# Decoder block on one core: pair operands summed by accumulating transfers, two branch units interleaved, operand work spread over six plain feed-forward pairs

## The chip, the cores and the metric

The kernel runs on one core of a Trainium2 chip. The metric is the device time of one execution in microseconds; before the change it is 979.95 us, the median of 3 runs (978.97 to 980.76). TensorE is called PE here, its weight loads PEld, VectorE DVE, ScalarE ACT, GpSimd POOL, and SP is SyncE, which only issues transfers.

## What is computed

One hybrid decoder block for 512 tokens of width 1024, with 16 learned meta tokens in front (528 columns in all):

```python
xn   = rmsnorm(h, norm1_g)
proj = xn @ w_in            # mq mk mv mi mf mo | gq gk gv ga gr | gate_m gate_g
mqk  = silu(causal_depthwise_conv(concat(mq, mk)))
y_m  = head_rmsnorm(mlstm_chunkwise(mq, mk, mv, logi, logf)) * sigmoid(mo)
y_g  = head_rmsnorm(gla_chunked(gq, gk, gv, loga)) * silu(gr)
merged = sigmoid(gate_m) * (y_m @ w_branch_m) + sigmoid(gate_g) * (y_g @ w_branch_g)
h  = h + merged @ w_out
hn = rmsnorm(h, norm2_g)
h  = h + (silu(hn @ w_ff_gate) * (hn @ w_ff_up)) @ w_ff_down
out = rmsnorm(h, final_g)
```

## The kernel before

**Layout and precision.** Features lie on the 128 partitions and tokens along the free dimension. The big products are made in float32r, as three passes: each operand is split into a high part (a cast on ACT) and a low part (operand minus high part, a subtraction on DVE), and `mm3` (lines 298 to 303) issues high x high, high x low and low x high. The low part of a weight tile is made in `wlo` (L192), the high part in `whi` (L187).

**Units and pairs.** A unit is one weight tile of 1024 x 128, so 8 steps k of `mm3`. `job_list` (L52) writes out the order of all units by hand: gates; four heads of mq, mk, mv, mv, mo, mo; then gm, the GLA projections gq, gk, gv, gr, the branches bm and bg, gg, out, the feed-forward units fg and fu, and down. Some jobs are pairs (`pair`, L350): two weight tiles at once by a scheme of seven half-size products in place of eight, named q1, q5, q6, p2, p3, p4, p7 (`seven`, L339). A pair is 84 matmuls of 256 columns (272 with the meta tokens), where two plain units have 48 of 512. The product p3 of a pair is left pending and issued inside the next job (`left`, `PENDING`, L305). In the feed-forward stage the first NSTD = 5 pairs of fg and fu are plain units, the other 17 are pairs.

**Who sets the order.** The program is unrolled, and each engine works through its own instructions in the order in which they were written. Side work is held in Python generators (`side`, and `mixers` of which only the first runs). After each k of a unit, and after every second k of a pair's product, `tick` (L152) lets every generator go one step; `yield n` means that the generator goes on n ticks later. So a generator's yields decide where among the matmuls its ACT, DVE and DMA instructions stand. `begin` (L270) issues the raw weight load of the fifth unit ahead on SP and places the splits of coming weights at fixed k of the present unit. There are four raw buffers, so a load waits until the low part of an earlier tile is made.

**Operands of the pairs.** A pair needs sums and differences of blocks of the activations, split in two parts. For the mixer's pairs, `normed_x` (L504) makes the normed x from mv 1 on, k by k; `mixed_x` (L520), started at mv 4, adds high and low parts back (L538, L540), forms the sums (L542, L543, L548, L551) and splits them in 272-column halves (`two`, L569: ACT L577, DVE L578 and L575). For the feed-forward pairs, `operands` (L1268) runs from the second unit on: it makes the normed rows `hx` (L1292) and the sums and splits (`two`, L1275), one tick between most steps; the loop at L1345 ticks on until all are there. Weights need such sums as well: accumulating transfers on POOL (L182, L211) make some of them.

**Branches.** `branch_unit` (L1121) runs one unit of bm or bg. Its `need` splits the operand for k and k + 1 just before use (`joined`, `parts`, L838 on ACT and L839 on DVE). Two operands of bg are split earlier, during the last gg pair (`all_parts`, L842). `head_out` (L782) makes these operands per head; its last step is L827.

**Small work on POOL.** `conv` clears three columns there (L704), `mlstm` copies a selector (L862), and `swiglu` (L1251) multiplies there in the plain feed-forward pairs (L1260).

Of the kernel before, what the change touches and what calls it, by code (L numbers as in the profile page):

```python
# [15 lines left out]
P = 128  # L16
D = 1024
KT = 8
# [4 lines left out]
H = 4  # L23
# [22 lines left out]
NSTD = 5  # L46
# [54 lines left out]
def hybrid_block(ctx: ExitStack, tc: tile.TileContext, xT, wst, par, con, out):  # L101
# [35 lines left out]
    X = Box()  # L137

# [131 lines left out]
    def begin(*names):  # L270
# [10 lines left out]
        if all(i[0] == "s" for i in ITEMS[n - 2:n + 1]) and len(names) == 1:  # L281
            n += 1
# [24 lines left out]
    def unit(name, outs, ah, al, need=None):  # L307
# [3 lines left out]
        for k in range(KT):  # L311
            if need is not None:
                need(k)
# [13 lines left out]
    def unit_real(name, ah=None, al=None, need=None):  # L327
# [5 lines left out]
        unit(name, [(o, 0, NS)], ah, al, need)  # L333
# [170 lines left out]
    def normed_x():  # L504

        nh, nl = [], []
        for k in range(KT):
# [4 lines left out]
            S.copy(hi, t)  # L512
            yield 3
# [6 lines left out]
    def mixed_x():  # L520
# [5 lines left out]
        X.w = {n: ([], []) for n in SEVEN}  # L526
        for k in range(4):
            for j in range(2):
                p = (h, l)[j]
                X.w["p2"][j].append(p[k + 4][:, c1])  # L530
                X.w["p3"][j].append(p[k + 4][:, c2])
        three = lambda a: a.rearrange("p (j n) -> p j n", j=2)
        for k in (0, 2):
            t1, t3 = tt(n=2 * HA), tt(n=2 * HA)
            for j in range(2):
                b1, b2 = tt(), tt()
                u1, u3 = three(t1)[:, j], three(t3)[:, j]
                V.tensor_tensor(b1, h[k + j].bitcast(F32), l[k + j].bitcast(F32), ALU.add)  # L538
                yield 1
                V.tensor_tensor(b2, h[k + 4 + j].bitcast(F32), l[k + 4 + j].bitcast(F32), ALU.add)  # L540
                yield 1
                V.tensor_tensor(u1, b1[:, c1], b1[:, c2], ALU.subtract)  # L542
                V.tensor_tensor(u3, b2[:, c2], b1[:, c2], ALU.subtract)  # L543
                yield 1
                two("q5", u1, j)
                yield 1
                two("p7", u3, j)
                V.tensor_tensor(u1, u1, b2[:, c2], ALU.add)  # L548
                yield 1
                two("q6", u1, j, True)  # L550
                V.tensor_tensor(u3, u1, b2[:, c1], ALU.subtract)  # L551
                yield 1
                two("p4", u3, j)
                yield 1
        while unit_ix[0] < UNITS.index(("mo", 7)):
            yield 1
        for k in (0, 2):
            for j in range(2):
                t = tt(F32R, 2 * HA)
                for i in range(2):  # L560
                    c = slice(i * HA, (i + 1) * HA)
                    S.copy(t[:, c], (h, l)[j][k + i][:, c1])
                    X.w["q1"][j].append(t[:, c])
                yield 1
        X.ready = True

    mixed = {}

    def two(n, src, j, neg=False):  # L569
        if j == 0:  # L570
            mixed[n] = tt(F32R, 2 * HA), tt(F32R, 2 * HA)
        hi, lo = (a[:, j * HA:(j + 1) * HA] for a in mixed[n])
        if neg:
            act(hi, src, AF.Copy, scale=-1.0)
            V.scalar_tensor_tensor(lo, src, -1.0, hi.bitcast(F32), ALU.mult, ALU.subtract)  # L575
        else:
            S.copy(hi, src)  # L577
            V.tensor_tensor(lo, src, hi.bitcast(F32), ALU.subtract)  # L578
        X.w[n][0].append(hi)
        X.w[n][1].append(lo)  # L580
# [121 lines left out]
    def conv(box, ps, m, isk):  # L702
        raw = tt(n=TW)
        G.memset(raw[:, 0:3], 0.0)  # L704
# [854 lines left out]
```

## Time and profile before

| | before |
|---|---|
| median of 3 runs | 979.95 us |
| the profiled execution, its own time | 979.11 us |
| its span, first to last instruction | 977.3 us |
| mean granted PE clock | 0.983 |
| DMA, share of 16 engines by queue | hardware 32.5%, software (POOL) 12.7% |

Start of some stages in the profiled execution, in us from the span's start: mv 5 123.0, mo 5 135.6, mo 6 183.3, first gm pair 207, bm 0 299.7, bg 0 511.7, out 0 564, fg 0 608.6, first feed-forward pair 672.9, down 841.6.

The profile's rows name the line of the kernel that issued an instruction, its engine, and its output and inputs by the program's names, so `b<-t,whi` is a matmul into a bank from an activation tile and a weight's high part. "A <- B" in the list of waits says that A stood idle until B was done.

### The profile page before, as it was taken

Reading aid. Unit: us, or ns where it says so; the run is one execution under the profiler, and the core shown is the slowest. Engines: PE = TensorE matmul, PEld = TensorE weight load, DVE = VectorE, ACT = ScalarE, POOL = GpSimd, SP = SyncE. Lnnn points to the kernel's source line nnn. Section 1 sums busy time; section 2 is a strip of 40 time slices with the busy share of each in tenths; the row PEclk is TensorE's granted clock in tenths of the full one; section 3 lists DMA queues with packets and bytes.
Section 4 is the critical chain, followed back from the end, with each engine's and each line's share of the span. In section 5 each row is a group of like instructions: output and inputs, shape, how many; then the busy total and the mean of one; then the engine's idle time right before and its main releaser. Section 6 shows DMA issues by size and latency. Waiting matters only on the chain.

```text
span 977.3 us, 15554 instructions
## 1 busy us (share of the span) xinstructions
PE 926.2 (95%) x6119; PEld 847.9 (87%) x6119; DVE 649.5 (66%) x970; ACT 547.5 (56%) x957; POOL 78.2 (8%) x107
## 2 busy tenths in 40 slices
PE   6999989789999999999998999979999999999995
PEld 6989978778998889999996888858999999988885
DVE  6897787657865567776876555775777777852423
ACT  7557776768865346766873334534555555731321
POOL 0010000001110001101100000012211111000000
PEclk9999998989999999999999999989999999999998
DMA  7342211244563356656642334235777877323302
GB/s 260 102 113 73 87 55 54 65 109 111 139 153 95 97 129 163 158 135 141 140 130 78 105 129 141 65 109 121 193 182 186 187 187 164 109 87 107 107 2 87
DMA packets 43578, 118.64 MB, mean 121 GB/s; under 512 B 4976, under 2 KB 7024, under 8 KB 43504
## 3 DMA queue, kind: packets, MB, share of 16 engines
q1 hardware_dynamic: 31760, 97.19, 32.5%
q0 software_dynamic: 10656, 19.40, 12.7%
q8 instruction: 48, 0.79, 0.3%
q10 hardware_dynamic: 1088, 1.05, 0.3%
q14 instruction: 26, 0.21, 0.1%
HBM read 115.52 MB, written 2.10 MB: 120 GB/s over the span
## 4 chain that ended last, share of the span: by engine, by line
PE 71%; DVE 13%; ACT 12%; issue 2%; DMA 1%; SPq 0%; DVEq 0%; ACTq 0%
PE b L345 11%; PE b L302 11%; PE b L303 11%; PE b L347 11%; PE b L346 11%; PE b L301 11%; ACT t L132 5%; DVE wlo L192 2%; ACT whi L187 2%; ACT L132 1%; DVE t L713 1%; ACT L130 1%; PE b L1046 1%; PE b L1048 1%; DMA t<-xT 1%
## 5 line engine op out<-in xcount | busy, mean ns | idle before, releaser
L302 PE MATMUL b<-t,whi 128*128 128x512 f32 (+2 forms) x806 | 285.3, 354 | 6.3 <-DVE t L839 5.3
L301 PE MATMUL b<-t,whi 128*128 128x512 f32 (+2 forms) x758 | 269.1, 355 | 8.0 <-ACT t L132 6.7
L303 PE MATMUL b<-t,wlo 128*128 128x512 f32 (+2 forms) x758 | 265.8, 351 | 5.2 <-DVE wlo L192 5.2
L345 PE MATMUL b<-t,whi 128*128 128x256 f32 (+1 forms) x888 | 257.0, 289 | 6.7 <-ACT t L405 5.1
L347 PE MATMUL b<-t,wlo 128*128 128x256 f32 (+1 forms) x888 | 252.0, 284 | 0.0
L346 PE MATMUL b<-t,whi 128*128 128x256 f32 (+1 forms) x888 | 251.7, 283 | 0.0
L192 DVE TENSOR_TENSOR wlo<-raw,whi 128x1024 fp32r<-128x1024 f32 x155 | 188.9, 1222 | 52.6 <-ACT whi L187 52.5
L187 ACT CAST whi<-raw 128x1024 fp32r<-128x1024 f32 x155 | 161.6, 1046 | 70.7 <-PE b L346 28.8
L302 PEld LDWEIGHTS b<-t,whi 128*128 128x128 f32 x806 | 153.3, 190 | 29.5 <-DVE t L839 7.5
L345 PEld LDWEIGHTS b<-t,whi 128*128 128x128 f32 x888 | 168.7, 190 | 8.8 <-ACT t L405 6.2
L301 PEld LDWEIGHTS b<-t,whi 128*128 128x128 f32 x758 | 144.9, 191 | 28.1 <-ACT t L132 6.7
L346 PEld LDWEIGHTS b<-t,whi 128*128 128x128 f32 x888 | 168.8, 190 | 0.4
L347 PEld LDWEIGHTS b<-t,wlo 128*128 128x128 f32 x888 | 168.4, 190 | 0.0
L303 PEld LDWEIGHTS b<-t,wlo 128*128 128x128 f32 x758 | 144.4, 191 | 25.2 <-DVE wlo L192 6.1
L132 ACT ACTIVATE t<-t 128x512 f32<-128x512 f32 (+4 forms) x118 | 67.2, 590 | 26.9 <-DVE t L655 6.8
L182 POOL DMA_DIRECT2D raw<-wst x37 | 32.1, 867 | 372.8 <-DMA wf<-wst 107.2
L187 ACT CAST whi<-wf 128x1024 fp32r<-128x1024 f32 x37 | 38.9, 1051 | 21.4 <-PE b L346 14.0
L132 ACT ACTIVATE t<-f 128x256 f32<-128x256 f32 (+1 forms) x24 | 11.6, 481 | 61.7 <-DVE f L1406 61.7
L192 DVE TENSOR_TENSOR wlo<-wf,whi 128x1024 fp32r<-128x1024 f32 x37 | 45.1, 1218 | 0.0
L345 PE MATMUL b<-t,wgh 128*128 128x256 f32 (+1 forms) x148 | 42.5, 287 | 0.0
L347 PE MATMUL b<-t,wgl 128*128 128x256 f32 (+1 forms) x148 | 42.4, 286 | 0.0
L346 PE MATMUL b<-t,wgh 128*128 128x256 f32 (+1 forms) x148 | 42.2, 285 | 0.0
(223 smaller groups left out, 1194.1 us busy)
## 6 DMA issues: line engine op xcount, KB each, us to landing
raw<-wst SPq DMA_DIRECT2D x155, 512.0 KB, 3.7
wf<-wst SPq DMA_DIRECT2D x37, 256.0 KB, 3.2
wf<-wst POOLq DMA_DIRECT2D x37, 256.0 KB, 5.6
raw<-wst POOLq DMA_DIRECT2D x37, 256.0 KB, 4.9
t<-xT SPq DMA_DIRECT2D x8, 264.0 KB, 5.7
t<-xT SPq DMA_DIRECT2D x8, 256.0 KB, 3.9
out<-t SPq DMA_DIRECT2D x4, 256.0 KB, 2.4
out<-t ACTq DMA_DIRECT2D x4, 256.0 KB, 2.6
```

Source lines behind the costliest of these rows:

```text
L130: S.preload_act_table_set(want)
L132: S.activation(o, i, func, **kw)
L182: G.dma_start(lr(r, 0), lr(wst[v - 1], 0), accum_op=ALU.add)
L187: S.copy(t, src)
L192: V.tensor_tensor(t, src, hi.bitcast(F32), ALU.subtract)
L301: T.matmul(o, w_h, ah[:, c0:c1], start=first, stop=False)
L302: T.matmul(o, w_h, al[:, c0:c1], start=False, stop=False)
L303: T.matmul(o, w_l, ah[:, c0:c1], start=False, stop=last)
L345: T.matmul(o, h, xh_[k][:, c0:c1], start=start and k == 0, stop=False, skip_group_check=not start)
L346: T.matmul(o, h, xl_[k][:, c0:c1], start=False, stop=False, skip_group_check=not start)
L347: T.matmul(o, l, xh_[k][:, c0:c1], start=False, stop=k == 3, skip_group_check=not start)
L713: V.scalar_tensor_tensor(a, raw[:, i + c0:i + c0 + n], pr[:, col + i:col + i + 1], a, ALU.mult, ALU.add)
```

## The change

1. `normed_x` also writes the normed x (`pos`) and its negative (`neg`, 272 columns) to memory. `mixed_x` runs twice side by side, each for two k: it loads blocks from there, and POOL's accumulating transfers form the sums; the splits are made 544 columns wide.
2. The first two units of bm and of bg run interleaved, k by k (`first_two`); the high and low parts are issued at different steps (`part`), and four operands of bm are split during the gm pairs.
3. NSTD goes from 5 to 6, and `operands` issues its steps two or three ticks apart, high and low part at different steps.
4. `conv`'s memset goes from POOL to DVE, `mlstm`'s selector copy from POOL to ACT.

```diff
-NSTD = 5
+NSTD = 6
...
-    def begin(*names):
+    def begin(*names, more=True):
...
-        if all(i[0] == "s" for i in ITEMS[n - 2:n + 1]) and len(names) == 1:
+        if all(i[0] == "s" for i in ITEMS[n - 2:n + 1]) and len(names) == 1 and more:
...
             S.copy(hi, t)
+            neg = tt(n=HA)
+            act(neg, t[:, 256:] if k < 4 else t[:, :HA], AF.Copy, scale=-1.0)
+            nc.sync.dma_start(X.pos[k // 2][k % 2], t)
+            nc.sync.dma_start(X.neg[k // 2][k % 2], neg)
             yield 3
...
+    def mixed_x(i):
...
+        def two(n, src, neg=False):
+            hi, lo = tt(F32R, 2 * HA), tt(F32R, 2 * HA)
+            if neg:
+                act(hi, src, AF.Copy, scale=-1.0)
+            else:
+                S.copy(hi, src)
+            yield 2
+            if neg:
+                V.scalar_tensor_tensor(lo, src, -1.0, hi.bitcast(F32), ALU.mult, ALU.subtract)
+            else:
+                V.tensor_tensor(lo, src, hi.bitcast(F32), ALU.subtract)
...
+        t1, t3 = tt(n=2 * HA), tt(n=2 * HA)
+        plus = lambda t, m, c: G.dma_start(three(t), mem(m, c), accum_op=ALU.add)
+        nc.sync.dma_start(three(t1), mem(X.pos[i], c1))
+        nc.sync.dma_start(three(t3), mem(X.pos[i + 2], c2))
+        yield 4
+        plus(t1, X.neg[i], c1)
+        plus(t3, X.neg[i], c1)
+        yield 16
+        yield from two("q5", t1)
+        yield 1
+        plus(t1, X.pos[i + 2], c2)
+        yield from two("p7", t3)
+        del t3
+        yield 14
+        yield from two("q6", t1, True)
+        yield 1
+        plus(t1, X.neg[i + 2], c1)
+        yield 16
+        yield from two("p4", t1)
...
-        G.memset(raw[:, 0:3], 0.0)
+        V.memset(raw[:, 0:3], 0.0)
...
+    def part(y, k, j):
+        if j == 0:
+            hi = hpool[0].tile([P, NS], F32R, tag="h", name=nm("h")) if k < 6 and y is ym else tt(F32R, NS)
+            S.copy(hi, y[k])
+            y[k] = y[k], hi
+        else:
+            s, hi = y[k]
+            lo = tt(F32R, NS)
+            V.tensor_tensor(lo, s, hi.bitcast(F32), ALU.subtract)
+            y[k] = hi, lo, True
...
-        G.tensor_copy(sel, cn[:, NS + h:NS + 8:H].unsqueeze(2).to_broadcast([P, 2, P]))
+        S.copy(sel, cn[:, NS + h:NS + 8:H].unsqueeze(2).to_broadcast([P, 2, P]))
...
+    def first_two(names, y):
+        (u, s0), (v, s1) = begin(names[0], more=False), begin(names[1], more=False)
+        w = splits.pop(u), splits.pop(v)
+        os = bank(), bank()
+        for k in range(KT):
+            for j in (k, k + 1, k + 2):
+                if j < KT and (j == k or y[j] is not None):
+                    joined(y, j, j < k + 2)
+            for o, ws in zip(os, w):
+                mm3(o, ws, k, y[k][0], y[k][1], 0, NS, k == 0, k == KT - 1)
+            for q in (2 * k, 2 * k + 1):
+                left(*PENDING.get(q, ()))
+                for f in (s0, s1)[q // 8].get(q % 8, ()):
+                    f()
+                tick()
+        return os
...
                 if what == "gg" and i == 6:
-                    run(all_parts(yg, 2))
+                    run(some_parts(yg, 2))
+                elif what == "gm" and i == 4:
+                    run(some_parts(ym, 4))
...
             elif i == 4:
-                run(mixed_x())
+                run(mixed_x(0))
+                run(mixed_x(1))
...
                     V.scalar_tensor_tensor(b[:, j], hres[m + j], pr[:, C_N2 + m + j:C_N2 + m + j + 1], rs2.v,
                                            ALU.mult, ALU.mult)
-                    yield 1
+                    yield 3
...
+            a = high("q1", b11)
             V.tensor_tensor(t1, b11, b12, ALU.subtract)
+            yield 2
+            low(*a)
+            a = high("q5", t1)
+            yield 2
             V.tensor_tensor(t3, b22, b12, ALU.subtract)
+            yield 2
+            low(*a)
+            a = high("p7", t3)
+            yield 2
             V.tensor_tensor(t1, t1, b22, ALU.add)
+            yield 2
+            low(*a)
+            a = high("q6", t1, True)
+            yield 2
             V.tensor_tensor(t3, t1, b21, ALU.subtract)
+            yield 2
+            low(*a)
+            a = high("p4", t3)
+            b = high("p2", b21)
+            yield 3
+            low(*a)
+            a = high("p3", b22)
+            yield 2
+            low(*b)
+            yield 2
+            low(*a)
+            yield 2
```

More of the change, by code (lines that the diff above doesn't have):

```diff
@@ L305, in hybrid_block, with unit @@
     PENDING = {0: ["s5"], 1: ["mid", "c22"], 2: ["p3"], 3: ["c12"], 5: ["fin"]}
-    def unit(name, outs, ah, al, need=None):
+    def unit(name, outs, ah, al):
         u, steps = begin(name)
@@ L332, in unit_real @@
             return o, scale
-        unit(name, [(o, 0, NS)], ah, al, need)
+        unit(name, [(o, 0, NS)], ah, al)
         return o
@@ L555, in mixed_x @@
+        yield from two("q6", t1, True)
[3 more added lines that the diff above has]
+        yield from two("p4", t1)
+        del t1
         while unit_ix[0] < UNITS.index(("mo", 7)):
             yield 1
[L557 to L580, printed above, removed]
+        for j in range(2):
+            t = tt(F32R, 2 * HA)
+            for k in ks:
+                c = slice((k % 2) * HA, (k % 2 + 1) * HA)
+                S.copy(t[:, c], (h, l)[j][k][:, c1])
+                X.w["q1"][j][k] = t[:, c]
+            yield 1
@@ L845, in all_parts @@
                 yield 1
-            parts(y, k)
+            part(y, k, 0)
             yield 1
+            part(y, k, 1)
+            yield 2
     WOFF = []
@@ L1058, in box @@
         return b
-    X.h, X.l, X.scale, X.ready = xh, xl, None, False
+    X.h, X.l, X.scale, X.ready = xh, xl, None, 0
+    xdram = ctx.enter_context(tc.tile_pool(name="xdram", bufs=4, space=bass.MemoryType.DRAM))
+    X.pos = [xdram.tile([2, P, NT], F32, tag="pos", name=nm("pos")) for _ in range(4)]
+    X.neg = [xdram.tile([2, P, HA], F32, tag="neg", name=nm("neg")) for _ in range(4)]
     ps_g = unit_all(("gates", 0))
@@ L1118, in joined @@
         if not isinstance(y[k], tuple):
-            parts(y, k)
-    def branch_unit(name, y):
-        h, l = [None] * 8, [None] * 8
-        def need(k):
-            for j in range(k, min(k + 2, KT)):
-                if y[j] is not None or j == k:
-                    joined(y, j)
-                    h[j], l[j] = y[j]
-        return unit_real(name, h, l, need)
+            part(y, k, 0)
+        if j and len(y[k]) == 2:
+            part(y, k, 1)
+    def first_two(names, y):
[14 more added lines that the diff above has]
+        return os
+    duo = {}
+    def branch_unit(name, y):
+        what, i = name
+        if i == 0:
+            duo[what] = first_two((name, (what, 1)), y)
+        if i < 2:
+            return duo[what][i]
+        return unit_real(name, [a[0] for a in y], [a[1] for a in y])
     ALL, REAL = (0, HA), (NM, HA)
@@ L1178, in hybrid_block @@
         elif what == "bm":
[L1179 to L1182 removed]
+            while not hpool:
+                tick()
             run(branch(merged[i], branch_unit(job[0], ym), gm[i]))
@@ L1273, in operands, with high, low @@
             xw[n] = [], []
[L1275 to L1277 removed]
+        three = lambda a: a.rearrange("p (j n) -> p j n", j=2)
+        def high(n, src, neg=False):
+            hi = tt(F32R, NS)
             if neg:
[L1279 to L1286 removed]
+                act(three(hi), src, AF.Copy, scale=-1.0)
+            else:
+                S.copy(three(hi), src)
+            xw[n][0].extend(three(hi)[:, j] for j in range(2))
+            return n, src, hi, neg
+        def low(n, src, hi, neg):
+            lo = tt(F32R, NS)
+            if neg:
+                V.scalar_tensor_tensor(three(lo), src, -1.0, three(hi).bitcast(F32), ALU.mult, ALU.subtract)
+            else:
+                V.tensor_tensor(three(lo), src, three(hi).bitcast(F32), ALU.subtract)
+            xw[n][1].extend(three(lo)[:, j] for j in range(2))
         for k in (0, 2):
```

96 lines of the change are left out of this document (23 added, 73 removed).

## The prediction

> **What bounds the kernel now.** I read the page first, then the waits of the PE, then the granted clock by stretch, then stretches with and without waits, then the groups and the order of single instructions in the stretches that lose time.
>
> ```profile
> span 977.3 us, 15554 instructions
> PE 926.2 (95%) x6119; PEld 847.9 (87%) x6119; DVE 649.5 (66%) x970; ACT 547.5 (56%) x957; POOL 78.2 (8%) x107
> ```
>
> The PE is the bound: 95% of the span. Only two things can shorten the run: fewer matmul columns, or fewer waits of the PE. The waits, longest in total first (columns: total us, times, longest):
>
> ```profile
> PE b L302 <- DVE t L839: 5.3, 6, 2.9
> PE b L303 <- DVE wlo L192: 5.2, 2, 3.6
> PE b L345 <- ACT t L405: 5.1, 4, 2.7
> PE b L745 <- DVE wl L907: 4.9, 1, 4.9
> PE b L935 <- DVE t L920: 2.7, 1, 2.7
> PE b L930 <- DVE wl L907: 1.2, 1, 1.2
> PE b L866 <- ACT t L132: 1.2, 1, 1.2
> PE b L806 <- DVE t L802: 0.5, 1, 0.5
> ```
>
> Nearly all end on DVE or ACT, so on operands that were made late. L839 is the low part of a branch operand, L192 the low part of a weight, L920 the low part of the mLSTM denominator. A wait has a second price, the clock behind it (columns: stretch, its us, then busy us and count of PE, PEld, DVE, ACT, POOL, then the granted clock, DMA share and GB/s):
>
> ```profile
> 144.96:151.79 6.83, 4.49 (x12) 3.80 (x13) 4.78 (x12) 2.53 (x5) 0.00 (x0) 0.50 0.23 77
> 189.33:192.75 3.42, 3.22 (x10) 2.74 (x11) 2.92 (x10) 1.88 (x7) 1.40 (x2) 0.50 0.43 69
> 213.23:220.05 6.82, 6.16 (x27) 5.97 (x28) 2.19 (x4) 3.42 (x11) 0.00 (x0) 0.50 0.51 132
> 516.90:520.40 3.50, 3.50 (x16) 3.31 (x15) 0.89 (x2) 0.84 (x3) 0.00 (x0) 0.52 0.00 0
> 646.72:653.55 6.83, 4.54 (x11) 3.57 (x12) 5.80 (x8) 3.79 (x5) 0.00 (x0) 0.50 0.43 125
> ```
>
> In each of these five stretches the clock is half, and half of the PE's busy time in it is lost too. Each stands at one of the waits above of 2.7 us or more. The Trainium skill ("TensorE: Matmul & The Clock Gate", Why this matters for your kernels) says that idle gaps above about 3 us bring the half clock. The trace is stricter: waits of 2.7 and 2.9 us brought it. By the page's rule I would not count the clock at 144.96 and at 516.90 (2.2 and 1.8 us) as won with those waits, and the gain below would be some 3 us smaller; I go by the rows.
>
> What undisturbed work costs, and three stretches that the change touches:
>
> ```profile
> 126.00:162.00 36.00, 30.64 (x176) 26.49 (x175) 29.07 (x64) 23.42 (x50) 0.00 (x0) 0.91 0.16 53
> 511.60:525.40 13.80, 9.76 (x39) 7.27 (x39) 9.27 (x14) 7.57 (x13) 0.00 (x0) 0.88 0.31 87
> 531.00:564.20 33.20, 33.20 (x145) 27.04 (x145) 19.82 (x25) 9.43 (x12) 0.00 (x0) 1.00 0.35 105
> 636.60:656.50 19.90, 13.94 (x50) 10.30 (x48) 17.53 (x24) 9.18 (x13) 2.21 (x3) 0.83 0.32 95
> 656.50:667.50 11.00, 11.00 (x50) 9.01 (x49) 5.86 (x6) 2.74 (x4) 4.26 (x4) 1.00 0.54 126
> 693.50:833.00 139.50, 139.50 (x1179) 139.50 (x1178) 100.61 (x141) 79.47 (x141) 22.57 (x26) 1.00 0.76 180
> ```
>
> A plain unit (24 matmuls of 512 columns) takes 33.2/6 = 5.53 us, in the feed-forward stage 11.0/2 = 5.50; a tick, one k of it, is 0.69 us. A feed-forward pair (84 matmuls of 256 columns) takes 139.5/14 = 9.96 us, so 0.119 us a matmul.
>
> **The change part by part.**
>
> **Feed-forward operands.** 636.6 to 656.5 holds the units fu 2 and fg 3: 19.9 us for work of 11.0, a loss of 8.9. The cause is DVE, busy 17.5 of these 19.9 us.
>
> ```profile
> L192 DVE TENSOR_TENSOR wlo<-raw,whi 128x1024 fp32r<-128x1024 f32 x6 | 7.2, 1218 | 1.0 <-ACT whi L187 1.0
> L1292 DVE SCALAR_TENSOR_TENSOR hx<-f,pr,t 128x512 f32<-128x512 f32 x8 | 5.6, 746 | 0.0
> L1283 DVE TENSOR_TENSOR t<-t,t 128x512 fp32r<-128x512 f32 x6 | 4.1, 685 | 0.2
> ```
>
> The operands need 8 x 0.746 (L1292) plus 14 low parts and 8 sums at 0.685: 21.0 us of DVE. The old generator issues them in 2 x 12 = 24 ticks, 16.6 us of PE time. To these come 3 low parts of weights (3.7) and 3 pairs of swiglu products (L1255 and L1256, at the same 0.685 some 2 us in this stretch): 27 us into 16.6. The weights' low parts stand behind them in DVE's queue, and the PE waits for L192. The new generator takes 2 x 35 = 70 ticks, 48 us. It begins at tick 6 of fu 0 and ends at tick 74 of the 88 that the six plain pairs offer from there. DVE then has 21.0 + 8.75 x 1.218 + 4.4 x 1.37 = 38 us in 48, 79%: the low parts keep their place, and I count nothing for them. If that cover fails, the price is a share of the 8.9. I leave 0.3 us standing. The sixth plain pair costs 11.0 - 9.96 = 1.04 us. Gain 8.9 - 1.04 - 0.3 = 7.6 (bounds 4 and 7.9).
>
> One rule speaks against this part.
>
> ```profile
> 643.75 1.59 POOL L1260 TENSOR_TENSOR t<-t,t 128x512 f32<-128x512 f32 x1 [16.02 <-ACT t L132]
> 644.24 1.65 DVE L1308 TENSOR_TENSOR t<-t,hx 128x512 f32<-128x512 f32 x1
> ```
>
> Beside POOL's product, DVE's sum took 1.65 us in place of the 0.685 of its like. The new kernel has six such products, and more DVE sums around them: up to 6 x 0.97 = 5.8 us more of DVE, 91% of the 48 us. It still fits, with less room. The Trainium skill ("SBUF — State Buffer", Who interferes with whom) states the cause, a DVE instruction with two SBUF inputs against a GpSimd instruction that reads SBUF; the trace agrees.
>
> **First two units of bg side by side.** The order around bg 0 (start us, us, instruction):
>
> ```profile
> 511.65 0.39 PE L301 MATMUL b<-t,whi 128*128 128x512 f32 x1
> 512.21 1.14 ACT L838 CAST t<-h 128x512 fp32r<-128x512 f32 x2
> 514.36 1.28 DVE L827 TENSOR_TENSOR h<-t,t 128x512 f32<-128x512 f32 x2
> 515.56 0.68 DVE L839 TENSOR_TENSOR t<-h,t 128x512 fp32r<-128x512 f32 x1
> 516.30 0.50 PE L302 MATMUL b<-t,whi 128*128 128x512 f32 x1 [2.87 <-DVE t L839]
> ```
>
> From 511.6 to 525.4 stand one plain unit and the last twelve matmuls of the pair before (the pending p3): 5.53 + 12 x 0.119 = 6.96 of 13.8 us, a loss of 6.8. The PE eats one k in 0.69 us, and a k needs 0.57 on ACT and 0.68 on DVE, behind the two L827 of the last head. Side by side a k lasts 1.38 us. The low part of k = 2 is then wanted after 12 matmuls, p3 and one more: 511.65 + 2.77 + 1.42 + 0.23 = 516.07. DVE delivers at 516.24, since nothing ahead of it in its queue changes. A wait of 0.2 us is left, no half clock, and from there supply is twice as fast as demand, except around the last pair's two sigmoids on ACT. I leave 1.1 of the 6.8: gain 5.7 (bounds 3.4 and 6.8). Branch results come up to 5.5 us later; nothing waits for them before out 0, seven units on. Two units open at once hold one more bank of eight. Both begin calls come at the start, so the second unit's raw load is issued eight ticks earlier and the weights' splits stand at the ticks they had: nothing.
>
> **The same for bm, and four operands early.**
>
> ```profile
> PE b L302 <- DVE t L839: 1.6, 3, 0.8
> ```
>
> That is the wait from 299 to 319 us. Four of eight operands are now split during gm 4 to 7, when ym has long been complete; the rest has double time. Gain 1.5 (bounds 0 and 2.2).
>
> **Mixer operands through memory.** mixed_x runs from tick 1 of mv 5, which begins at 123 us.
>
> ```profile
> L578 DVE TENSOR_TENSOR t<-t,t 128x272 fp32r<-128x272 f32 x12 | 5.3, 439 | 5.8 <-ACT t L577 5.8
> L538 DVE TENSOR_TENSOR t<-t,t 128x528 f32<-128x528 f32 x4 | 2.8, 700 | 0.0
> L542 DVE TENSOR_TENSOR t<-t 128x272 f32<-128x272 f32 x4 | 1.7, 434 | 0.0
> L551 DVE TENSOR_TENSOR t<-t,t x4: 430/436/438, 136.9 to 162.8; 128x272 f32<-128x272 f32 x4
> ```
>
> DVE loses 16 low parts (0.439), 8 sums of 528 columns (0.700; L538 and L540) and 16 of 272 (0.434; L542, L543, L548, L551): 19.6 us. It gets 8 low parts of 544 columns, not in the trace: between 0.70 (L538) and 0.88 (two of 272). I take 0.71, being nearest to the 528-column row: 5.7 us. So 14 us leave a stretch in which DVE is busy 29.07 of 36 us. There the PE waits at L930, L935, L866 and L806, 5.6 us, and loses 4.49/2 = 2.2 to the clock: 7.8. But the new low parts stand at ticks 23 to 26, in mo 5, just where L935 waits, so I take 5 (bounds -3 and 7.8). The waits at L745 (189 us) and L345 (214 us) I leave as they are: the old mixed_x ended at 163 us (its last sums, L551, start at 162.8), and there ACT is late by itself. The new q6 and p4 parts, at ticks 40 and 59, now lie ahead of them: 2.8 us of DVE and as much of ACT, in queues that at that time also stand idle.
>
> The new transfers:
>
> ```profile
> L211 POOL DMA_DIRECT2D wf<-wst x37 | 33.4, 910 | 88.0 <-DMA wf<-wst 30.1 <-ACT t L410 15.4 <-ACT wgh L252 11.7
> wf<-wst POOLq DMA_DIRECT2D x37, 256.0 KB, 5.6
> 115.61 0.33 SPq L180 DMA_DIRECT2D raw<-wst  x1
> SPq L180 <- DVE wlo L192: 65.6, 8, 12.3
> ```
>
> An accumulating transfer of 128 rows of 2 KB takes POOL 0.91 us and lands after 5.6. One of 272 KB in 256 rows: between these and twice these, 1.82 and 11.2; I take 1.2 and 6.5. The longest run is four in a row: 4 x 1.2 + 6.5 = 11.3 us from the fifth tick of mv 5; the first copy of a sum stands 16 ticks later, near 143 us, so 4 us or more of cover. If it failed, ACT would stand at that copy, with the high parts of weights and the mLSTM's exponentials behind it, and the PE behind those. On POOL only later accumulations of weights stand behind the sums, the first at tick 40. SP runs ahead of the PE: the raw load issued at the head of mv 5 started at 115.61, so the plain loads behind it are early by 7 us. The sixteen writes of pos and neg stand in SP's queue between raw loads, which wait up to 12.3 us for a free buffer; no PE wait in the list ends on a raw load, so one copy of ACT more in front of them is covered. I count nothing. The eight neg copies (0.42 each by the 272-column rows) come in normed_x, 3.4 us of ACT over 50 us; nothing to 0.5. The memsets of conv (to DVE) and sel (to ACT) move 0.1 to 0.4 us each off POOL, so that they do not stand behind its transfers: nothing.
>
> **Sum.** 7.6 + 5.7 + 1.5 + 5.0 = 19.8 us. The profiled execution took 979.1 us (its span 977.3 and 1.8 around it), 0.8 below the median: 979.1 - 19.8 + 0.8 = 960.1, so 960.
>
> **The rivals.**
>
> *The mixer stage gives nothing.* ACT, not DVE, is the late engine there, or the later q6 and p4 lengthen the wait at L745 by up to 3 us. For it: L745 and L345 wait in a stretch without mixed_x. Against it: L935 and L930 end on DVE. Time 965 to 968.
>
> *The mixer stage gives more.* With DVE in time, the waits at 189 and 214 us and their clock go too: 4.9 + 1.6 + 2.7 + 3.1 = 12.3. If half to all of that comes, 948 to 954. Against it: their cause lies on ACT.
>
> *The spreading doesn't do all it says.* A low part still comes late in the feed-forward stage (by the port rows above), or bg keeps half its loss: 3 to 4 us less, 963 to 965.
>
> *The transfers come late (slower).* If SP issues the first loads behind the raw load that waits 12.3 us, they land near 139, and at the upper bounds the fourth sum lands 4 x 1.82 + 11.2 = 18.5 later, 157; ACT's queue stands at the copy, due at 143, for 14 us, and in the two later rounds (2 x 1.82 + 11.2 = 14.8 us in 13) for 2 each. With three spells of half clock at 2.2 that is 24.6 lost in place of 5 won: 960.1 + 5 + 24.6 = 989.7. It ends slower than before from 15 us of such losses on, the sum of the other parts. Against it: 115.61.
>
> **How the numbers follow.** The forecast 960 (956 to 962 by its terms) gets 0.48; nothing in the mixer stage 0.22; more there 0.15; half-done spreading 0.10; late transfers 0.05. The range 949 to 969 leaves out the late transfers and the best third of the cascade, and takes in the rest. About 0.2% can be told from no change here. Faster 0.94, same 0.01, slower 0.05.
>
> **What would show it.** Right: 608 to 842 us shortened by 7 to 8 with no PE wait at L192's rows; no half clock at 517 and 647; L930 and L935 without waits of over 1 us; waits at L745 and L345 still there. Wrong: ACT idle in front of a copy that reads a sum, ended by a DMA; PE waits for the low parts of the new branch routine; DVE above 90% in the new plain pairs.

## The result and the profile after

The changed kernel takes 948.41 us, the median of 4 runs (947.62 to 948.94), against 979.46 for the kernel before beside it: a ratio of 0.9687, interval 0.9663 to 0.9711. It gains 31.0 us where I forecast 19.8, and its time lies 0.6 below my range. Its profiled execution took 948.5, span 946.7.

The page of after, first lines, and then its waits of the PE (total us, times, longest):

```profile
span 946.7 us, 15478 instructions
PE 917.5 (97%) x6083; PEld 842.3 (89%) x6083; DVE 636.2 (67%) x940; ACT 546.2 (58%) x954; POOL 86.8 (9%) x102
```

```profile
PE b L302 <- ACT t L132: 6.6, 1, 6.6
PE b L344 <- ACT t L404: 6.1, 4, 3.6
PE b L875 <- ACT sel L872: 1.9, 1, 1.9
PE b L939 <- DVE t L757: 1.6, 1, 1.6
...
PE b L748 <- ACT t L591: 0.5, 1, 0.5
```

The first of these is the program's start. Lines have moved: L344 was L345, L748 was L745, L843 was L839, L193 was L192. Of the waits that the prediction showed, those at L192, L930 and L935 are gone, and of those at L839 0.3 us is left; the one at L345 stands; and the one at L745, 4.9 us, is down to 0.5. That last one I had left standing.

Where the time went, stretch by stretch (windows from the first matmul of a job to that of the next; busy us and count of PE, PEld, DVE, ACT, POOL, then clock, DMA share, GB/s). Before: mo 5, mq 3, mo 6, bm 0, bg 0, and three plain feed-forward pairs from fg 2:

```profile
135.63:153.70 18.07, 13.88 (x64) 11.24 (x63) 15.24 (x38) 8.98 (x21) 0.00 (x0) 0.81 0.18 58
153.70:183.27 29.57, 27.53 (x214) 26.41 (x212) 18.81 (x32) 19.63 (x39) 1.07 (x3) 1.00 0.23 63
183.27:207.11 23.84, 18.90 (x91) 15.75 (x90) 15.81 (x29) 17.86 (x38) 1.40 (x2) 0.93 0.30 77
299.74:352.29 52.55, 51.27 (x243) 41.71 (x244) 26.98 (x38) 18.83 (x27) 1.72 (x2) 1.00 0.36 96
511.89:564.23 52.34, 48.30 (x206) 38.63 (x205) 32.14 (x43) 18.27 (x27) 0.00 (x0) 0.97 0.30 88
631.11:672.88 41.77, 35.81 (x146) 28.23 (x145) 29.39 (x38) 16.42 (x24) 6.69 (x6) 0.92 0.40 113
```

The same six after:

```profile
136.35:147.51 11.16, 11.16 (x63) 9.70 (x62) 6.74 (x13) 7.27 (x13) 2.41 (x2) 1.00 0.54 150
147.51:174.24 26.73, 26.73 (x213) 26.38 (x212) 20.09 (x32) 23.36 (x43) 3.34 (x3) 1.00 0.50 98
174.24:192.07 17.83, 17.38 (x91) 14.49 (x90) 12.10 (x23) 14.26 (x34) 0.88 (x1) 1.00 0.25 56
...
285.06:335.65 50.59, 50.55 (x243) 41.77 (x242) 25.37 (x35) 18.43 (x26) 1.72 (x2) 1.00 0.37 103
495.20:541.56 46.36, 46.10 (x205) 37.28 (x204) 31.86 (x43) 18.32 (x27) 0.00 (x0) 1.00 0.35 104
608.51:641.85 33.34, 33.34 (x145) 27.06 (x144) 27.93 (x36) 15.99 (x24) 8.71 (x4) 1.00 0.41 119
```

In five of the six the PE is now busy for all but 0.3 us, at full clock; in the third it idles 0.45. The counts of matmuls agree to within one, so what was gained here came from waits, from the clock behind them and from small gaps between matmuls. By the prediction's parts:

| part | forecast | measured in the profiled executions |
|---|---|---|
| feed-forward, fg 0 to down | 7.6 | 233.0 to 225.8: 7.2 |
| bg | 5.7 | 52.3 to 46.4: 6.0 |
| bm | 1.5 | 52.6 to 50.6: 2.0 |
| mixer operands | 5.0 | mo 5 6.9, mq 3 2.8, mo 6 6.0, first gm pairs -0.6: 15.2 |

These make 30.4 of the span's 30.6. Three parts came to within 0.5 us. The mixer part gave three times its forecast, and the experiments are about it.

### The profile page after: what moved, and what is told of

The parts are those of the page before. It is cut to its first block, busy times and chain, and to the rows that moved or that the text cites. A ratio compares the mean times of both kernels' runs of the same rounds, so it can differ in the third digit from the quotient of the medians.

```text
span 946.7 us, 15478 instructions
## 1 busy us (share of the span) xinstructions
PE 917.5 (97%) x6083; PEld 842.3 (89%) x6083; DVE 636.2 (67%) x940; ACT 546.2 (58%) x954; POOL 86.8 (9%) x102
## 4 chain that ended last, share of the span: by engine, by line
PE 78%; ACT 9%; DVE 8%; issue 3%; DMA 1%; DVEq 0%; SPq 0%; ACTq 0%
PE b L303 13%; PE b L302 13%; PE b L304 13%; PE b L344 12%; PE b L345 11%; PE b L346 11%; ACT t L132 4%; ACT whi L188 2%; DVE wlo L193 1%; ACT L130 1%; PE b L1056 1%; DVE t L716 1%; PE b L1058 1%; PE b L1035 1%; ACT L132 1%
## 5 line engine op out<-in xcount | busy, mean ns | idle before, releaser
L303 PE MATMUL b<-t,whi 128*128 128x512 f32 (+2 forms) x822 | 289.9, 353 | 1.0 <-DVE t L471 0.7
L302 PE MATMUL b<-t,whi 128*128 128x512 f32 (+2 forms) x774 | 274.0, 354 | 6.7 <-ACT t L132 6.6
L304 PE MATMUL b<-t,wlo 128*128 128x512 f32 (+2 forms) x774 | 270.8, 350 | 0.0
L344 PE MATMUL b<-t,whi 128*128 128x256 f32 (+1 forms) x864 | 250.0, 289 | 7.7 <-ACT t L404 6.1
L346 PE MATMUL b<-t,wlo 128*128 128x256 f32 (+1 forms) x864 | 245.1, 284 | 0.0
L345 PE MATMUL b<-t,whi 128*128 128x256 f32 (+1 forms) x864 | 245.0, 284 | 0.0
L193 DVE TENSOR_TENSOR wlo<-raw,whi 128x1024 fp32r<-128x1024 f32 x155 | 193.1, 1249 | 50.8 <-ACT whi L188 50.5
L344 PEld LDWEIGHTS b<-t,whi 128*128 128x128 f32 x864 | 164.3, 190 | 9.9 <-ACT t L404 7.2
L345 PEld LDWEIGHTS b<-t,whi 128*128 128x128 f32 x864 | 164.3, 190 | 0.5
L304 PEld LDWEIGHTS b<-t,wlo 128*128 128x128 f32 x774 | 146.8, 190 | 19.9 <-DVE wlo L193 0.3
L132 ACT ACTIVATE t<-t 128x512 f32<-128x512 f32 (+6 forms) x124 | 70.4, 588 | 29.8 <-DVE t L1289 9.3
L212 POOL DMA_DIRECT2D wf<-wst x36 | 32.5, 912 | 155.3 <-DMA wf<-wst 85.7
L193 DVE TENSOR_TENSOR wlo<-wf,whi 128x1024 fp32r<-128x1024 f32 x36 | 43.9, 1218 | 0.0
L1456 DVE TENSOR_TENSOR f<-f,b 128x512 f32<-128x512 f32 (+1 forms) x9 | 5.7, 629 | 53.3 <-PE b L304 53.3
L344 PE MATMUL b<-t,wgh 128*128 128x256 f32 (+1 forms) x144 | 41.0, 285 | 0.0
```

Source lines behind the costliest of these rows:

```text
L132: S.activation(o, i, func, **kw)
L193: V.tensor_tensor(t, src, hi.bitcast(F32), ALU.subtract)
L212: G.dma_start(lr(st.f, 1), lr(wst[u + 1], 1), accum_op=ALU.add)
L302: T.matmul(o, w_h, ah[:, c0:c1], start=first, stop=False)
L303: T.matmul(o, w_h, al[:, c0:c1], start=False, stop=False)
L304: T.matmul(o, w_l, ah[:, c0:c1], start=False, stop=last)
```

## The experiments

Times are medians where an interval stands, else of one execution; the kernel before took 979.2 to 979.7 beside them. "Lag" below is the time from the end of a unit's matmuls (units counted off in their order) to the start of ACT's copy that empties its bank (L588, after L591). The cuts of code show an edit in part, some of them against the kernel of an earlier experiment, which the text then names.

**Each half alone.** First the mixer part and the moves off POOL, without the rest:

> The kernel before with the mixer operands alone changed (sums through memory, memset and selector copy moved off POOL); branches and feed-forward stage as before. Theory A (carried lag): mixed_x's DVE work makes DVE and ACT late, and the PE pays for that lag twice, in mo 5 and again at the transposes of mo 6, so the stretch from mv 5 to the first gm pair goes from 84 to about 68 us and the time to about 964. Theory B (as predicted: the wait in mo 6 is ACT's own): only the waits in mo 5 and mq 3 go, 5 to 8 us, the wait of 4.9 us at the transposes stays, 972 to 975.

```diff
-                run(mixed_x())
+                run(mixed_x(0))
+                run(mixed_x(1))
```

(into the kernel before, with `normed_x` and `mixed_x` as after.)

Measured 964.53, ratio 0.9855 (0.9833 to 0.9877): 14.9 us. From mv 5 to mo 6 its stretches equal after's within 0.01 us. So the large gain belongs to the mixer part and needs nothing from the other two. The rest alone:

> The changed kernel with the old mixed_x (sums on DVE, nothing through memory); branches, feed-forward stage and the two small moves as changed. Theory A: the whole 15 us come back, about 964, with waits at the denominator in mo 5 and at the transposes in mo 6 (some 5 us). Theory B: what went in mo 6 went by one of the other edits, so it stays away: about 954 to 956, no wait of over 1 us in mo 6.

```diff
-                run(mixed_x(0))
-                run(mixed_x(1))
+                run(mixed_x())
```

(into the kernel after, with `normed_x` and `mixed_x` as before.)

Measured 962.93. The wait in front of the transposes is back (L743, 5.0 us), mo 5 is 5.9, mq 3 5.0 and mo 6 6.4 longer than after. The two halves add up.

**Is it DVE's load?** My working took the gain from 14 us of DVE work that leave. Here the changed kernel also makes the 24 old sums on DVE, in the first 36 ticks of the old place; nothing uses them:

> The changed kernel, with the 24 old sums (8 of 528 columns, 16 of 272, about 12.6 us of DVE) issued on DVE at the ticks that they had before, their results unused. The memory route stays. Theory A: the load alone brings the waits back: 3 to 7 us in mo 5 and 4 to 5 us at the transposes in mo 6, 957 to 963. Theory B: waits in mo 5 only, 951 to 955. If it is not load but the place of the splits, nothing returns: 948 to 950.

```diff
+    def ballast():
...
+                V.tensor_tensor(b1, h[k + j].bitcast(F32), l[k + j].bitcast(F32), ALU.add)
+                yield 1
...
+                run(ballast())
```

Measured 948.51, as without them, but that is in part luck: from mv 5 to the first gm pair this kernel takes 2.2 us more than after (mq 3 1.3, mo 6 1.0, mo 5 nothing), and its first gm pairs take 2.5 less, since the half clock that after has there did not come (last section). A window of this kernel, and of the kernel before, over the same 39 us (columns as above):

```profile
123.00:162.00 39.00, 37.95 (x253) 34.82 (x252) 35.85 (x68) 31.26 (x62) 8.01 (x7) 1.00 0.54 115
```

```profile
123.00:162.00 39.00, 33.63 (x201) 29.49 (x200) 31.22 (x66) 26.40 (x56) 0.00 (x0) 0.91 0.17 54
```

DVE works more here than in the kernel before, 35.85 against 31.22 us, and yet the PE gets 253 matmuls through in place of 201. Load on DVE did not make the waits of mo 5. Half of these sums, started when mo 5 is done (unused too; the cut is against the kernel with all of them):

> The changed kernel, with half of the old sums (about 6.3 us of DVE, results unused) issued from mq 3 on, over 18 ticks, so that they end two units ahead of mo 6. Theory A: no wait in mo 5; the lag of ACT and DVE behind the PE rises by 3 to 6 us in mk 3, is carried, and the PE waits for it at the transposes of mo 6: 951 to 955. Theory B: the queues work it off before mo 6, 948 to 950.

```diff
+        while unit_ix[0] <= UNITS.index(("mq", 3)):
+            yield 1
...
-        for k in (0, 2):
+        for k in (0,):
```

Measured 950.7: mo 6 is 1.8 longer, with 2.2 us of wait in front of the transposes. So load can bring back part of that one wait. The time lies between the two ranges; the wait is the one that the theory of the carried lag named.

**Is it the order?** With the load ruled out for mo 5, what is left is that the old `mixed_x` writes a sum, the copy that reads it, the low part that reads the copy and the next sum directly one behind the other. Here are the engines' waits for each other in the kernel before from 123 to 162 us (A <- B: A stood idle until B was done; total, times, longest):

```profile
DVE t L578 <- ACT t L577: 5.8, 7, 2.9
...
ACT t L132 <- DVE t L548: 3.5, 3, 1.4
...
ACT t L577 <- DVE t L551: 2.9, 3, 1.1
ACT t L577 <- DVE t L542: 2.8, 1, 2.8
```

DVE waits for a copy, ACT for a sum, in turn: 15.0 us in four rows, all of them lines of mixed_x. Each time the queue behind waits too. After has no such row. Two kernels form the sums on DVE again, with no transfers, spread over 54 ticks, and differ only in where the steps stand. With dependent steps a tick or more apart:

> The kernel of the second experiment (all changed but the mixer operands), with the sums on DVE as before, but each sum, the high part that reads it and the low part that reads that stand one to four ticks apart, in 544-column splits, over 54 ticks; nothing goes through memory. Theory A (load): DVE carries the sums again, so some 955 to 963, with waits in mo 5 and mo 6. Theory C (order): what costs is that a sum, its high part and its low part stood next to each other in two in-order queues, each of which then stands at its head for the other; apart, they cost nothing, and the time is 948 to 952.

```diff
-        nc.sync.dma_start(three(t1), mem(X.pos[i], c1))
...
+            V.tensor_tensor(u1[:, j], b1[j][:, c1], b1[j][:, c2], ALU.subtract)
+            V.tensor_tensor(u3[:, j], b2[j][:, c2], b1[j][:, c2], ALU.subtract)
+            yield 2
...
         yield from two("q5", t1)
```

(`two` leaves 2 ticks between the copy and the low part)

and with them adjacent (against the kernel with the steps apart):

> As the experiment before it: the same sums and splits on DVE, the same widths, the same 54 ticks; only here high and low part stand in one tick, and each sum directly ahead of its high part, as before the change. Theory A (load): the same time as the kernel with the steps apart. Theory C (order): 4 to 14 us more than that one, with ACT waiting for sums and DVE for high parts, and PE waits in mo 5 or mo 6.

```diff
-            yield 2
...
-        yield from two("q5", t1)
-        yield 1
+        two("q5", t1)
+        yield 7
```

Apart: 953.84, ratio 0.9738 (0.9722 to 0.9754); mo 5 and mq 3 take 11.9 and 26.9 us, 0.9 above after. Adjacent: 959.27; mo 5 and mq 3 take 17.2 and 29.1, much like the kernel before. Same instructions, same ticks in all: the adjacent order costs 7.5 us in these two units, 2.7 of them by half clock (144 to 151 us, 5.3 us of PE time). But it is bunched as well: three of the four splits of a half stand within three ticks, and 12 ticks without any follow. No run separates the two. And apart costs something too: 953.84 lies above the 948 to 952 that I expected of the order alone. The waits of the adjacent kernel from 123 to 162 us show engines standing for each other again (L546 is the copy, L563, L570 and L574 sums):

```profile
ACT t L132 <- DVE t L570: 1.5, 1, 1.5
ACT t L546 <- DVE t L574: 1.5, 1, 1.5
ACT t L546 <- DVE t L563: 1.4, 1, 1.4
```

The kernel with the steps apart has one row of this kind, of 1.4 us.

What "apart" does not bring is the wait of mo 6: 4.5 us in front of the transposes. A kernel with the sums apart in 34 ticks, to be done long before mo 6, was to settle that (the cut is against the one in 54 ticks):

> As the kernel with the sums on DVE and dependent steps apart, but in 34 ticks in place of 54, so that the sums are done well ahead of mo 6. Theory that load close ahead of mo 6 makes the wait there: the wait in front of the transposes falls from 4.5 us to 1.5 or less, the stretch from mo 6 comes within 2 us of the changed kernel's, mo 5 and mq 3 lose 1 to 3 by the tighter order, and the time is 948 to 951. Rival, the sums' own chain makes the wait: the stretch from mo 6 stays 5 longer than the changed kernel's, and the time at 953 to 956.

```diff
-            yield 2
-        yield 2
+            yield 1
...
-        yield 4
+        yield 3
```

Measured 958.65, ratio 0.9791 (0.9775 to 0.9808): neither theory. mq 3 takes 31.8 us, 5.0 over after, and the wait in mo 6 is 5.0. Its list has ACT and DVE waiting for each other again (L546 is a copy, L551 its low part, L576 a last sum, L958 a step of the mLSTM on DVE):

```profile
ACT t L132 <- DVE t L958: 5.1, 1, 5.1
DVE t L551 <- ACT t L546: 3.3, 2, 2.1
...
ACT t L546 <- DVE t L576: 2.6, 2, 1.4
```

As I read it, one tick (0.69 us) between dependent steps is no distance when the queues run further behind than that; the lags below are several us. The counterpart, the sums unused but in the 54 ticks of the "apart" kernel:

> The changed kernel with the 24 old sums on DVE, results unused, but at the ticks of the fifth experiment (over 54 ticks, until the end of mv 7), where the third had them over 36. It tells what made the wait of 4.5 us in mo 6 in the fifth. If it is DVE load close ahead of mo 6: the lag of ACT at the end of mv 6 goes from 7.6 to 10 us or more, and the PE waits 3 to 4.5 us in mo 6, 950 to 954. If it is ACT copies standing at sums (there are none here): lag below 9 us, a wait of 0.5 to 1.5 us, 946 to 950.

```diff
-                yield 3
-                V.tensor_tensor(u1, u1, b2[:, c2], ALU.add)
+            yield 5
+            for j in range(2):
+                V.tensor_tensor(u1[:, j], u1[:, j], b2[j][:, c2], ALU.add)
```

(against the kernel with the extra sums above; they now stand in the ticks of the kernel with dependent steps apart.) Measured 955.45, over what either theory allowed: mo 5 and mq 3 lose 0.2 and 1.7, mo 6 loses 6.6, its wait is 4.9. Nobody reads these sums, so for the wait of mo 6 no chain through them is needed; for mo 5 they do next to nothing. That it is their load on DVE that acts in mo 6 doesn't follow, as the end of the next part shows.

**The wait of mo 6.** In the kernel before, ACT ahead of the transposes, and the transposes (start us, us, instruction):

```profile
184.01 1.28 ACT L132 ACT_TABLE_LOAD   x1
185.30 1.16 ACT L132 ACTIVATE t<-t 128x512 f32<-128x512 f32 x2
186.48 1.28 ACT L130 ACT_TABLE_LOAD   x1
...
189.12 0.63 ACT L588 COPY t<-b 128x264 f32<-128x264 f32 x2
```

```profile
184.19 0.40 PE L303 MATMUL b<-t,wlo 128*128 128x512 f32 x1
189.53 1.11 PE L745 MATMUL b<-pr,t 128*128 128x128 f32 x4 [4.94 <-DVE wl L907]
190.29 0.78 PE L301 MATMUL b<-t,whi 128*128 128x512 f32 x1
```

After, the same block on ACT and the same place of the PE:

```profile
172.97 1.28 ACT L130 ACT_TABLE_LOAD   x1
174.26 0.40 ACT L132 ACTIVATE t<-t,acol 128x128 f32<-128x128 f32 x1
...
175.61 0.63 ACT L591 COPY t<-b 128x264 f32<-128x264 f32 x2
```

```profile
175.17 0.40 PE L304 MATMUL b<-t,wlo 128*128 128x512 f32 x1
176.02 0.72 PE L748 MATMUL b<-pr,t 128*128 128x128 f32 x4 [0.45 <-ACT t L591]
```

The row names DVE's wl as the releaser, but in both kernels the transposes start as the first half of ACT's copy ends (189.5 and 176.0): they read what the copy writes. And in both the copy stands behind the same block of ACT work, table loads included. The difference is where the PE was: mv 6 ended 12.8 us ahead of the copy before (176.35), 7.65 after (167.96). The kernel writes the transposes 8 ticks behind the copy, and the wait is the lag less 7.2 to 8.2 us in eight of the kernels. The last column is how long ACT stands idle for the PE between its copies of mk 3 and mv 6:

| kernel | lag of mk 3 | lag of mv 6 | wait in mo 6 | ACT waits for PE |
|---|---|---|---|---|
| after | 2.0 | 7.65 | 0.45 | 0 |
| old sums early, unused | 2.9 | 8.6 | 1.4 | 0 |
| half of them, after mo 5 | 3.8 | 9.4 | 2.2 | 0 |
| sums unused, 54 ticks | 3.9 | 13.1 | 4.9 | 3.1 |
| all but the mixer part | 4.3 | 12.7 | 5.0 | 2.6 |
| sums on DVE, apart | 4.4 | 11.7 | 4.5 | 0.8 |
| sums apart, 34 ticks | 4.85 | 12.7 | 5.0 | 2.1 |
| before | 5.8 | 12.8 | 4.9 | 1.1 |

The kernel with adjacent sums has lags of 4.9 and 14.6, waits of 4.0 there and 2.1 just ahead, and 2.5 in the last column. In the first three rows the lag grows by 5.6 to 5.7 us from mk 3 to mv 6: a later mk 3 comes back in full as a later mv 6, so the lag is carried. In the other five it grows by more, and less the last column it is 5.7 to 6.5. So the second thing that makes the lag of mv 6 is a single wait of ACT for the PE, which none of the first three kernels has. Before, and with the sums unused in 54 ticks, it is this row:

```profile
178.08 0.83 ACT L132 ACTIVATE t<-t,pr 128x528 f32<-128x528 f32 x1 [1.11 <-PE b L888]
```

```profile
170.75 0.83 ACT L132 ACTIVATE t<-t,pr 128x528 f32<-128x528 f32 x1 [3.08 <-PE b L928]
```

After has it without a wait:

```profile
164.63 0.82 ACT L132 ACTIVATE t<-t,pr 128x528 f32<-128x528 f32 x1
```

L888 and L928 are matmuls of the mLSTM's scores. The activation reads no bank, so it doesn't wait for their result; as I read it, it writes a temporary tile (`tt`) whose buffer one of their operands still holds. The temporary tiles share 60 buffers (NTT), and the unused sums take from these too. So their harm in 54 ticks may come from buffers more than from load; the trace doesn't tell which buffer a tile has, and no run changes NTT.

If the wait in mo 6 is only the lag meeting a place in the order, then moving the place in the kernel before removes it:

> The kernel before, with the transposes of the last head's values written 6 ticks later (14 ticks after the second evacuation in place of 8). Theory of the carried lag: the evacuation of mv 6 comes 12.8 us after its unit's end in the kernel before, the transposes stand some 7.2 us behind that end in the PE's order, and the wait there is 4.9; six ticks are 4.1 us, so the wait falls to about 0.8 and the stretch from mo 6 to the first gm pair shortens by about 4, the time to 975 to 976. Rival, ACT by itself late behind the transposes' place wherever they stand, so that the wait only moves: the wait or those behind it stay at 4 to 5 in all, and the time at 978 to 980.

```diff
-            yield 8 if h or not need_lo else 16
+            yield (14 if h == 3 else 8 if h else 16) if need_lo else 8
```

Measured 972.7, below both ranges. The row in question:

```profile
189.69 0.72 PE L745 MATMUL b<-pr,t 128*128 128x128 f32 x4 [0.79 <-ACT t L588]
```

ACT's copy starts at 189.28, 0.16 later than before, the PE waits 0.79 in place of 4.94, the half clock at 189 is gone, mo 6 is 5.3 us shorter and the first gm pairs 1.0 longer; the rest of the 6.5 us lies in bg and the feed-forward units, where the half clock came for less long (none at 517 us, 3.4 us in place of 6.8 at 647), which the edit doesn't touch. So the wait is the lag meeting a place in the order, and the rival (the wait only moves) falls; where the lag comes from this run doesn't tell. One number in the kernel before was worth 5.3 of the 6.0 us that the mixer part gained in mo 6.

**The other pieces.** High and low parts at one tick, sums still through memory:

> The changed kernel with the memory route, but high and low part of each mixer operand in the same tick. Theory A: unchanged, 948 to 949. Theory C: DVE stands at eight low parts for ACT, whose lag is up to some microseconds; but no ACT copy waits for a DVE sum, so only part of the cost: 949 to 953.

```diff
                 S.copy(hi, src)
-            yield 2
```

Measured 944.88, below both theories; all stretches from mv 5 to mo 6 equal after's. The accumulating transfers have set the sums apart already, so the copy finds its input done. The 3.5 us below after come from the first gm pairs, below. The small work back on POOL:

> The changed kernel with conv's memset and the selector copy back on POOL. If the two moves are needed (POOL's queue stands at a sum that waits for DVE, and conv and the selector behind it): slower by 2 to 10 us, with PE waits at the selector matmul or ACT and DVE waits in conv. If they are worth nothing, as predicted: within 1.5 us of 948.4; the wait of 1.9 us at the selector in mv 2 then goes back to 0.7 us at acol.

```diff
-        V.memset(raw[:, 0:3], 0.0)
+        G.memset(raw[:, 0:3], 0.0)
-        S.copy(sel, cn[:, NS + h:NS + 8:H].unsqueeze(2).to_broadcast([P, 2, P]))
+        G.tensor_copy(sel, cn[:, NS + h:NS + 8:H].unsqueeze(2).to_broadcast([P, 2, P]))
```

Measured 949.36. The wait of 1.9 at L875 goes and two others of 0.8 and 1.1 stand in its place: nothing. The branches' first units one after the other, all else as after:

> The changed kernel with the first two units of bm and bg one after the other; the early splits of four operands of bm and two of bg, and high and low parts at different k, are kept. If side by side is what removed the wait, as predicted: bg loses 4 to 6 us, half clock included, bm up to 1 us, 953 to 956. If issuing the high part two k ahead is enough: 948 to 950.

```diff
-            for o, ws in zip(os, w):
-                mm3(o, ws, k, y[k][0], y[k][1], 0, NS, k == 0, k == KT - 1)
+            mm3(o, w, k, y[k][0], y[k][1], 0, NS, k == 0, k == KT - 1)
```

Measured 954.18; its waits:

```profile
PE b L303 <- DVE t L843: 4.4, 3, 2.9
```

bg is 4.0 longer than after, with half clock for 3.4 us at 502.5, and bm 1.7, where I expected up to 1: 5.7 of the 8.0 that both stretches gained is the interleaving, the rest the separate steps and early splits. Five plain pairs with the spread steps:

> The changed kernel with five plain pairs, the operands' steps as far apart as in the changed kernel. The operands end at tick 74 and five pairs offer 72, so the first pair waits for two or three ticks' work of DVE at most. If the sixth plain pair costs 1.04 us, as predicted, and the tail of the operands little: 947 to 948.5. If the tail is late: a PE wait at the first pair's p2 or p3 of 1 to 4 us, 949 to 952.

```diff
-NSTD = 6
+NSTD = 5
```

Measured 946.8. fg 5 and the stretch from fg 6 to down are 0.3 and 0.8 shorter and no wait comes back, so the sixth pair buys nothing: its price was 1.1, forecast 1.04.

**The clock ahead of the first gm pair.** The copies of q1 (on ACT ahead of that pair) on DVE, on top of the one-tick kernel:

> The kernel of the seventh experiment (memory route, high and low part in one tick), with the eight copies for q1 (272 columns, 2.6 us of ACT ahead of the first gm pair) on DVE. The wait left in the first gm pair ends on an ACT copy. If ACT's lag alone makes it: the wait falls from 2.8 to below 1 us, 941 to 944 in a run without half clock there. If ACT stands there for DVE or for its two table loads: wait and time as in the seventh, 945, or 948 with the half clock.

```diff
-                S.copy(t[:, c], (h, l)[j][k][:, c1])
+                V.tensor_copy(t[:, c], (h, l)[j][k][:, c1])
```

Measured 946.34, ratio 0.9669 (0.9653 to 0.9685); the wait there is 3.1 us where the one-tick kernel had 2.8. So q1 is not what that pair waits for. And all that seemed free put together (one tick, q1 on DVE, five plain pairs, the steps of hx 2 ticks apart; the cut shows two of these):

> The changed kernel with high and low parts of the mixer's pairs issued at one tick, the copies of q1 on DVE, and five plain feed-forward pairs in place of six (a step of hx every 2 ticks). By the single runs: the wait in front of the first gm pair 2.8 to 3.1 us with no half clock in most executions, fg 0 to down 0.9 shorter than the changed kernel's: 943.5 to 946, 2 to 4 below the changed kernel. If the half clock ahead of the first gm pair comes by the phase of its windows alone, the executions spread over 3 us. Rival: with five plain pairs the operands come late again at the first feed-forward pair, 947 to 950.

```diff
-NSTD = 6
+NSTD = 5
...
-                S.copy(t[:, c], (h, l)[j][k][:, c1])
+                V.tensor_copy(t[:, c], (h, l)[j][k][:, c1])
```

Measured 946.70, over the upper end of what I expected; ratio 0.9677 (0.9654 to 0.9699), four executions of 945.28 to 948.20. That is 1.7 below after with intervals that overlap: not shown to beat it. The executions fall in two groups, 945.3 and 945.5 with a mean clock of 0.996, 947.9 and 948.2 with 0.993. That is the next point.

## Why the prediction was wrong

**Feed-forward operands: right.** 7.2 for 7.6. From 608.51 to 641.85 the PE is busy throughout; DVE, 27.9 of 33.3 us, keeps the low parts of weights in their places at 84%. I had named a DVE above 90% as the sign of failure. The overlap with POOL costs about what the prediction allowed, but it meets the weights' low parts more than the sums:

```profile
620.42 1.69 POOL L1294 TENSOR_TENSOR t<-t,t 128x512 f32<-128x512 f32 x1 [5.49 <-ACT t L132]
620.87 2.33 DVE L193 TENSOR_TENSOR wlo<-raw,whi 128x1024 fp32r<-128x1024 f32 x1
```

Four low parts of weights beside a product took 1.85 to 2.33 us in place of 1.22, and one low part of an operand 1.62 in place of 0.68: 4.9 us of DVE against the 5.8 at most that I had named, and it fits. Only the sixth pair was not needed. The new generator also sets dependent steps apart, as in the mixer; that DVE was busy 17.5 of 19.9 us in the old stretch speaks for load as the cause here, but no run separates the two.

**bg and bm: right.** 6.0 and 2.0 for 5.7 and 1.5; no half clock near bg. The experiment puts 4.0 and 1.7 on the interleaving.

**Transfers and small moves at nothing: right, to 1 us.** One row of the profile for POOL's issue (us, mean ns), and the two of the issues (KB, median us to landing):

```profile
L555 POOL DMA_DIRECT2D t<-neg x6 | 7.3, 1367 | 44.6 <-DVE t L813 39.6 <-DVE t L547 3.9 <-DMA t<-neg 0.9
```

```profile
pos<-t SPq DMA_DIRECT2D x8, 264.0 KB, 2.3
...
t<-neg POOLq DMA_DIRECT2D x6, 272.0 KB, 6.3
```

I took 1.2 and 6.5 for the 272 KB; it is 1.37 and 6.3. No wait of ACT ends on a transfer in this stretch. The kernels that write pos and neg reach mv 5 at 123.6 to 123.8 us (124.4 with the small work on POOL), those that don't at 122.5 to 123.1: the writes and the neg copies cost some 0.5 to 1.3 there, of which I had allowed 0.5.

**Mixer operands: wrong, in two places.** The step that failed is "The waits at L745 (189 us) and L345 (214 us) I leave as they are: the old mixed_x ended at 163 us (its last sums, L551, start at 162.8), and there ACT is late by itself". The wait at L345 did stay (5.1 us before, 6.1 after). For L745 it doesn't hold, and that is 6.0 us (4.5 of wait, 1.6 of clock) of the 10.2 that the term lacks. ACT has its own block there, but that makes a lag of 7.65 us, which the 8 ticks cover but for 0.45. Of the other 5.1 us, 3.8 were brought along: they are there at mk 3 (5.8 against 2.0). 1.1 are the wait of ACT for the PE behind mk 3, which I had not seen. Here I read the end of a stretch of work as the end of its effect: mixed_x ended at 163 us, and its lag was still there at the copies of 175.6 and 189.1. The rival that has this cascade had the right time, 948 to 954, and I spoke against it with the same reason. It had it in part by luck: of the 12.3 us in its sum only the 6.0 at 189 us came, the wait and the half clock at 214 us stayed, and the rest is the second place.

The second place is the 5.0 itself: mo 5 and mq 3 gave 9.7, more than the bound of 7.8. I had summed the named waits and one stretch of half clock up to 162 us; the small gaps between matmuls and the rest of mq 3 were left out. And the reason beside it, 14 us less of DVE, isn't what did it. With that load put back mo 5 takes no longer, and the stretch to the first gm pair 2.2 us of the 15.8 gained up to there; with the load as it was and the order changed, most of the gain in mo 5 and mq 3 is there.

**What stays open.** Whether the wait of ACT for the PE behind mk 3 is one for a buffer, and why it comes in some orders and not in others. Whether adjacency or bunching made the waits of mo 5. That transfers are needed at all isn't shown either: with the sums on DVE the best order that I tried is 5.4 us slower, and its largest loss, 5.3 us, is in mo 6, where the six ticks might help; the two were not tried together.

## What to carry to other kernels

When two engines hand data to and fro in order, write a dependent step several ticks behind what it reads, and fill the ticks with other work: adjacent and bunched steps cost 7.5 us at equal load here. Before you call a late engine "late by itself", measure how far it ran behind at the last few points, and ask how much of that it brought along. In eight kernels here the wait of the PE for a copy was the copy's lag minus a nearly fixed distance in the order: try the distance first, since it is one number. And look in the late engine's own list for a wait that ends on the engine it serves: it may be one for a buffer.

## What the runs showed of the hardware

The half clock comes in steps of some 3.41 us (3.42, 6.82 and 6.83 us in the kernel before), and the same wait can bring none, one or two of them. Ahead of the first gm pair, after has this (wait of 3.6 us, then the stretch behind):

```profile
198.30:205.10 6.80, 5.39 (x23) 5.20 (x24) 2.94 (x5) 4.16 (x12) 0.00 (x0) 0.50 0.64 154
```

The kernel with the old sums unused has the same wait, and full clock:

```profile
PE b L344 <- ACT t L404: 6.0, 4, 3.6
```

```profile
196.00:203.00 7.00, 3.44 (x25) 2.96 (x24) 3.31 (x5) 6.96 (x13) 1.72 (x2) 1.00 0.68 131
203.00:210.00 7.00, 7.00 (x58) 6.91 (x57) 5.08 (x8) 6.16 (x14) 0.00 (x0) 1.00 0.30 95
```

The mixer part alone has it too, and 3.4 us of half clock behind it. The Trainium skill ("TensorE: Matmul & The Clock Gate", Part 1: The HAM clock gate) tells of a free-running window of some 3.4 us that decides, and these runs agree; its rule of gaps above about 3 us (Why this matters for your kernels) is looser than the kernel before, where a wait of 2.7 us brought 6.8 us of half clock at 213 us. So a wait near 3 us is worth its own length and then 0 to 3.4 us by the phase, which no change of the kernel aims at. The 3.5 us of the one-tick kernel, and the two groups of executions of the last one, are of that kind by their clock; a gain of that size at one such place isn't evidence for an edit.
